# Two of four weight sums of a seven-product matmul moved from VectorE to adding transfers

## The chip, the core and the metric

The kernel runs on one core of a Trainium2 chip. A core has five engines that run their own instruction streams and meet at semaphores: PE (TensorE, matrix products into PSUM), ACT (ScalarE), DVE (VectorE), POOL (GpSimd) and SP (SyncE, which in this kernel only issues transfers). Transfers between HBM and on-chip memory are carried by 16 DMA engines. The metric is the device time of one execution in microseconds, lower is better. The time before is 2126.88 us, the median of three runs (2124.67 to 2127.38).

## What is computed

Two layers of a streaming encoder over 256 positions of width 2048, in float32. The part that the change touches is the MLP of each layer:

```python
def sq_relu_mlp(h, g, w1, w2):
    a = jax.nn.relu(rms_norm(h, g) @ w1)     # 2048 -> 8192
    return (a * a) @ w2                      # 8192 -> 2048

h = h + o.reshape(B, S, D) @ a_w_out[l]
h = h + sq_relu_mlp(h, mlp_norm_g[layer], mlp_w1[layer], mlp_w2[layer])
```

Around it stand a forgetting attention (layer 1), one shared K/V projection, and a chunked attention with a relative bias (layer 2). Every weight is read from HBM once per execution.

## The kernel before

**Products.** A float32 product is made of three passes: weights and activations are each split into a rounded part `hi` and a remainder `lo`, and PE adds up hi times hi, hi times lo and lo times hi (lines 444, 446 and 448). For every weight tile of 128x1024 (a unit), ACT makes `hi` (line 210) and DVE makes `lo` (line 211). A helper, `fetch`, makes these splits for up to two units ahead of the one that PE multiplies, and keeps up to three loads ahead of that. A unit is 12 matmuls of 512 columns.

**Pairs.** The MLP is cut into 4 chunks of 2048 hidden columns. A chunk has four pairs: two that make hidden columns from `w1`, then two (the wide ones, `order == "wide"`) that multiply the hidden activations by `w2`. A pair makes two output blocks of 512 columns for two blocks of 128 positions. There are 16 pairs in each MLP, 32 in all, 16 of them wide. Of the 16 tiles of the inner dimension a pair sends some through a scheme of Strassen's kind, seven products instead of eight, and the rest (units `a2..a7`, `b2..b7`) through the plain way. In a wide pair these are six tiles (1536 weight columns for each quarter), in the others four (1024).

**Forms.** The seven products take the weight matrices 11, T3, T2, T1, 21, T4, 22 in this order (called f0 to f6 in the plan; in a wide pair each has a second, half-size part h0 to h6). 11, 12, 21 and 22 are quarters of the weights, brought from HBM by `bring`. The sums are T3 = 22 - 12, T2 = T3 + 11, T1 = 12 - 11, T4 = 21 - T2, each made by DVE at line 790 (`make`), in the room of a matrix that isn't needed any more: T2 in that of T3, T1 in that of 12, T4 in that of 11. Sums of the activations come from `sums` (lines 271 to 280, tiles `S` and `Sh`).

**Order of a wide pair.** f0 h0, a unit of the pair before (b5), f1 h1, b6, f2 h2, b7, f3 h3, a3, f4 h4, b3, f5 h5, a4, f6 h6, b4, a5, a6, a7; its own b5 to b7 fall into the next pair. T3 is made three or five units ahead of the pair (`prepare`, by the numbers `when`), T2 once T3 has been split (`issue`), T1 after b6, T4 after a3. Within each engine the written order is the order of execution (`keep_order`, for DVE, ACT, PE and SP; POOL isn't in it).

**PSUM.** A pair has four banks, `ps[0][0..1]` for its first block and `ps[1][0..1]` for its second. Before: form 0 goes to `ps[1][0]`, and ACT copies it to `ps[0][0]` (line 879). Form 1 goes to `ps[1][1]`, and ACT copies it to a tile `P7` (line 882), after b6. Forms 2, 3 and 6 go on adding to `ps[1][0]`. After h2 in a wide pair DVE writes `ps[0][1] = ps[1][0] + P7` (line 861), and form 3, which adds to `ps[1][0]`, waits until that has read it. After unit a3 DVE writes `ps[1][1] = ps[1][0] + P7` (line 865).

**Hidden activations.** When a block of hidden columns is complete, DVE turns it in 32x32 blocks (line 314), SP sends it to HBM (`turn<-z`, line 324) and fetches it back in another order (`q<-turn`, line 330). Then `take` makes relu on ACT (line 803), the square rounded to `hi` (808), the square itself (810), and on DVE the remainder `lo` (814, the step called low). These steps run after fixed units of the plan, set by the tuple `uses`, one for each of a chunk's four blocks n = 0 to 3. POOL has no work in the MLP.

Of the kernel before, what the change touches and what calls it, by code (L numbers as in the profile page):

```python
# [11 lines left out]
AF = mybir.ActivationFunctionType  # L12
ALU = mybir.AluOpType
# [19 lines left out]
WIDE = UN + 512  # L33
# [14 lines left out]
def trunk(ctx: ExitStack, tc: tile.TileContext, xT, xr, gs, hg, bf, wgate, w_in, w_oa, w1a, w2fa, w2sa,  # L48
          w_kv, w_qb, w_ob, w1b, w2fb, w2sb, rel, out):
    nc = tc.nc  # L50
    V, S, G, TE, SY = nc.vector, nc.scalar, nc.gpsimd, nc.tensor, nc.sync
# [144 lines left out]
    def issue(parts=1):  # L196
        form = None
        if not raws:
            load(parts)
        raw, cuts = raws.popleft()  # L200
        if not cuts:
            form, half = raw, raw.half
            raw, cuts = form.pair.t[form.name], [slice(0, 512 if half else UN)]
            if half:
                raw = raw[:, UN:]
        n = cuts[-1].stop
        hi = wsp.tile([P, n], F32R, name="hi" if n == UN else "hih", bufs=3 if n == UN else 1)
        lo = wsp.tile([P, n], F32R, name="lo" if n == UN else "loh", bufs=3 if n == UN else 1)
        for c in cuts:
            S.activation(hi[:, c], raw[:, c], AF.Copy)  # L210
            V.tensor_tensor(lo[:, c], raw[:, c], hi[:, c].bitcast(F32), op=ALU.subtract)  # L211
        ready.append((hi, lo, n < UN))
        if form and form.name == "T3" and half == form.pair.wide:
            make(form.pair, "T2")

    def half_next():
        u = raws[0][0] if raws else units[0]
# [29 lines left out]
    part = [None]  # L247
# [14 lines left out]
    def sums(a, fs, n=2):  # L262

        w = [wk.tile([P, 512], F32, name="sum", tag="wk") for _ in range(n)]

        def part(i):
            at = i * n * P
            v = w[at // 512][:, at % 512 : at % 512 + n * P].rearrange("p (g t) -> p g t", g=n)
            return v.rearrange("p g (i c) -> p g i c", i=4) if len(a[0][0].shape) == 4 else v

        V.tensor_tensor(part(0), a[1][0], a[1][1], op=ALU.add)
        V.tensor_tensor(part(1), part(0), a[0][0], op=ALU.subtract)
        V.tensor_tensor(part(2), a[0][0], a[1][0], op=ALU.subtract)
        V.tensor_tensor(part(3), a[0][1], part(1), op=ALU.subtract)
        hi, lo = ([fs[k][:, i * 512 : (i + 1) * 512] for i in range(n)] for k in range(2))
        for i in range(n):
            S.activation(hi[i], w[i], AF.Copy)
        yield
        for i in range(n):
            V.tensor_tensor(lo[i], w[i], hi[i].bitcast(F32), op=ALU.subtract)  # L280
        yield
# [185 lines left out]
    def form_products(ps, hi, lo, x, fs, i, half, stop):  # L467
        items = []
        for g in (2,) if half else range(2):
            if i in (0, 4, 5):  # L470
                xp = [x[2 * g + (i > 0)][:, k, (i == 5) * P : (i == 5) * P + P] for k in range(2)]
            else:
                c = {3: 0, 2: 1, 1: 2, 6: 3}[i]
                c = c * P if half else c * 256 + g * P
                xp = [fs[k + 2 * half][:, c : c + P] for k in range(2)]
            items.append((ps[i not in (4, 5)][i in (1, 5)], xp, g % 2, i < 2 and g == 0, i < 2 and g == stop))
        passes(items, hi, lo, skip_group_check=True)

    def panels(x, evacs, before=None, after=None, which=(None, None), tail=None):
# [301 lines left out]
    def make(p, name):  # L781
        t = p.t
        if name == "T3":
            t[name] = prob.tile([P, 9 * 3 * P], F32, name="wT3", tag="p", bufs=1) if p.order == "early" else room("bias", "wT3")
        else:
            t[name] = t[{"T1": "12", "T2": "T3", "T4": "11"}[name]]
        a, b, op = {"T1": ("12", "11", ALU.subtract), "T3": ("22", "12", ALU.subtract),
                    "T2": ("T3", "11", ALU.add), "T4": ("21", "T2", ALU.subtract)}[name]
        d, a, b = (t[i][:, : WIDE if p.wide else UN] for i in (name, a, b))
        V.tensor_tensor(d, a, b, op=op)  # L790

    def prepare(p, d):
        for name, at in zip(("12", "22", "21", "11", "T3", "T1"), p.units):
# [3 lines left out]
    def mlp(plan, x, Sx, st, last):  # L797
        base = turns[0]
        hids = [[] for _ in range(NCH)]
        Sh = [[] for _ in range(NCH)]  # L800

        def take(t, c, n):
            S.activation(t, t, AF.Relu)
            y = acts.tile([P, 2, GH, T], F32R, name="act")
            hi, lo = (y[:, i].rearrange("p k (b i c) -> p (k b) i c", b=NB, i=4) for i in range(2))
            t3 = t.rearrange("p (i kb c) -> p kb i c", i=4, c=32)
            yield
            S.activation(hi, t3, AF.Square)
            yield
            S.activation(t, t, AF.Square)  # L810
            yield

            def low():
                V.tensor_tensor(lo, t3, hi.bitcast(F32), op=ALU.subtract)  # L814

            hids[c].extend(y[:, :, j, :] for j in range(GH))
            low()
            yield
            if n == 0:
                r = prob.tile([P, 9 * 3 * P], F32R, name="Sh", tag="p", bufs=1)  # L820
                Sh[c].extend(r[:, i : i + n] for i, n in ((0, UN), (UN, UN), (2 * UN, 512), (2 * UN + 512, 512)))
                yield from sums([[t3[:, 2 * j + b :: 4] for j in range(2)] for b in range(NB)], Sh[c])
            elif n == 1:
                yield from sums([[t3[:, 2 * j + b : 2 * j + b + 1] for j in range(2)] for b in range(NB)], Sh[c][2:], 1)

        def turn_hidden(c, n):
            zt = []

            def f(b, ps):
                if b == 0:  # L830
                    zt.extend(turned("q"))
                blocks32(ps, zt[0], b)
                if b == NB - 1:
                    step = steps(lambda: take(zt[1], c, n))
                    uses = ((4, 5, 7, 8, 9, 10), (4, 5, 6, 7, 8, 9), (4, 5, 6, 8), (3, 4, 4, 5))[n]
                    if not c and n < 2:
                        uses = (4, 5, 6, 8, 9, 9) if n else (4, 4, 5, 6, 7, 8)
                    add_fill(carry(*zt, 0)[:2] + [[step] * uses.count(i) for i in range(3, uses[-1] + 1)])
            return f

        pairs = [p for p, q, u in plan if (q, u) == (2, 0)]

        def open_pair(p):
            m = pairs.index(p)
            c, second, r = m // 4, m % 4 >= 2, m % 2
            p.x, p.fs = (hids[c], Sh[c]) if second else (x, Sx)
            p.ps = [acc_pair(base), acc_pair(2 if p.third else 1 - base)]
            if second:
                p.evac = [(last if c == NCH - 1 else residual)(2 * r + q, st.r2) for q in range(2)]
            else:  # L850
                p.evac = [turn_hidden(c, 2 * r + q) for q in range(2)]

        starts = [i for i, it in enumerate(plan) if it[1:] == (2, 0)]
        for i, (p, q, u) in enumerate(plan):
            hi, lo = fetch()
            if p.ps is None:
                open_pair(p)
            if q > 1:
                form_products(p.ps, hi, lo, p.x, p.fs, u, q == 3, 1 + p.wide)
                if u == 2 and q == 2 + p.wide:  # L860
                    V.tensor_tensor(p.ps[0][1], p.ps[1][0], p.t["P7"], op=ALU.add)
            else:
                products(p.ps[q], hi, lo, p.x, u, not units and not ready, p.fast)
                if p.fast and (q, u) == (0, p.own):
                    V.tensor_tensor(p.ps[1][1], p.ps[1][0], p.t["P7"], op=ALU.add)
                    if p.wide:
                        make(p, "T4")
                run_fill()
                if u == KT // UA - 1:
                    for b in range(NB):  # L870
                        p.evac[q](b, p.ps[q][b])
                nxt = next((j for j in starts if j > i), None)
                if nxt is not None:
                    d = sum(1 for it in plan[i:nxt] if it[1] < 2)
                    prepare(plan[nxt][0], d)
            f, kind, k = plan[i - 1]
            if i and kind > 1 and kind == 2 + f.wide and k < 2:
                if k == 0:
                    S.activation(f.ps[0][0], f.ps[1][0], AF.Copy)
                else:  # L880
                    f.t["P7"] = wk.tile([P, 512], F32, name="p7", tag="wk")
                    S.activation(f.t["P7"], f.ps[1][1], AF.Copy)
                    make(f, "T1" if f.wide else "T4")

    st1, x1, S1 = RowStats("m"), [], []
    stage(o, [next_x(n, None, st1, 1, x1, fs=S1, then=st1.inverse if n == NG - 1 else None) for n in range(NG)], tail=tail_a, plan=plan_a)
# [126 lines left out]
```

## Time and profile before

| | |
|---|---|
| median of the runs | 2126.88 us |
| profiled execution, its own time | 2126.07 us |
| its span, first to last instruction | 2124.3 us |
| granted TensorE clock | 0.999 |
| PE busy | 2101.3 us (99%) |
| DVE busy | 1654.6 us (78%) |
| ACT busy | 1211.3 us (57%) |
| POOL busy | 49.1 us (2%) |
| bytes moved by transfers | 491.63 MB |

PE is busy nearly all the time, so what can be won without fewer products is PE's idle time, 23 us over the whole span. The view of waits tells which instruction ended such a wait, and the timeline shows the instructions of an engine in order of time, with the idle time ahead of one in square brackets behind it.

### The profile page before, as it was taken

To read this page: it belongs to the slowest core of one execution; us is meant where nothing else is said; L and a number is where in the kernel's file an instruction comes from. 1 tells how busy PE (TensorE), PEld (TensorE's weight loads), DVE (VectorE), ACT (ScalarE), POOL (GpSimd) and SP (SyncE) were. 2 spreads that over 40 slices of the span, in tenths; PEclk is the share of its full clock that TensorE was granted. 3 is DMA by queue.
4 is the path that set the end of the run, shared out by engine and by line. 5 is a ranking of instruction groups with operands and counts; after the bars stand their busy time and mean duration, and the time that the engine had idled before them with its cause. 6 is when DMAs were issued, how large, how long until landed. Compare 5 with 4: busy or idle time off the path is not lost.

```text
span 2124.3 us, 26113 instructions
## 1 busy us (share of the span) xinstructions
PE 2101.3 (99%) x9278; PEld 1729.3 (81%) x9278; DVE 1654.6 (78%) x1931; ACT 1211.3 (57%) x1519; POOL 49.1 (2%) x48
## 2 busy tenths in 40 slices
PE   9999999999999999999999999999999999999999
PEld 7888888877888887888788888888788878878887
DVE  5767776888788878878877677678887887888786
ACT  6544445665566566556575454456654655665664
POOL 1001000000000000000001010000000000000000
PEclk9999999999999999999999999999999999999999
DMA  8787788776676576477577777787766766765763
GB/s 281 244 249 243 224 264 255 238 246 210 220 256 206 200 265 228 170 239 269 181 240 261 234 228 235 239 276 237 247 211 217 241 203 222 248 212 195 261 234 129
DMA packets 179283, 491.63 MB, mean 231 GB/s; under 512 B 36416, under 2 KB 73424, under 8 KB 179152
## 3 DMA queue, kind: packets, MB, share of 16 engines
q1 hardware_dynamic: 179152, 489.96, 69.8%
q8 instruction: 73, 1.20, 0.2%
q14 instruction: 58, 0.48, 0.1%
HBM read 450.01 MB, written 39.87 MB: 231 GB/s over the span
## 4 chain that ended last, share of the span: by engine, by line
PE 84%; DVE 7%; DMA 4%; ACT 2%; issue 2%; SPq 1%; ACTq 0%; DVEq 0%
PE acc L446 23%; PE acc L448 23%; PE acc L444 23%; PE s L444 4%; PE s L446 4%; PE s L448 4%; DVE lo L211 3%; ACT hi L210 2%; DVE w L790 1%; DVE loh L211 1%; DMA q<-turn 1%; DMA turn<-z 1%; DMA raw<-in_w_in 1%; DVE wT L790 1%; PE s L583 1%
## 5 line engine op out<-in xcount | busy, mean ns | idle before, releaser
L211 DVE TENSOR_TENSOR lo<-raw,hi 128x1024 fp32r<-128x1024 f32 (+1 forms) x610 | 738.2, 1215 | 260.1 <-ACT hi L210 253.0
L210 ACT ACTIVATE hi<-raw 128x1024 fp32r<-128x1024 f32 (+1 forms) x610 | 640.8, 1053 | 367.3 <-PE acc L446 266.8
L444 PE MATMUL acc<-hi,act 128*128 128x512 f32 x2208 | 608.4, 394 | 2.0 <-ACT hi L210 1.1
L446 PE MATMUL acc<-hi,act 128*128 128x512 f32 x2208 | 599.7, 390 | 6.4 <-DVE act L814 6.4
L448 PE MATMUL acc<-lo,act 128*128 128x512 f32 x2208 | 598.4, 390 | 0.0
L446 PEld LDWEIGHTS acc<-hi,act 128*128 128x128 f32 x2208 | 413.4, 188 | 98.2 <-DVE act L814 10.7
L448 PEld LDWEIGHTS acc<-lo,act 128*128 128x128 f32 x2208 | 413.3, 188 | 89.0 <-DVE lo L211 3.2
L444 PEld LDWEIGHTS acc<-hi,act 128*128 128x128 f32 x2208 | 412.9, 188 | 87.9 <-ACT hi L210 2.1
L210 ACT ACTIVATE hi<-w 128x1024 fp32r<-128x1024 f32 x160 | 169.1, 1057 | 226.4 <-DVE w L790 105.2
L211 DVE TENSOR_TENSOR lo<-w,hi 128x1024 fp32r<-128x1024 f32 x160 | 194.8, 1218 | 83.9 <-ACT hi L210 83.8
L444 PE MATMUL s<-hi,act 128*128 128x512 f32 x416 | 112.6, 389 | 0.0
L446 PE MATMUL s<-hi,act 128*128 128x512 f32 x416 | 112.5, 389 | 0.0
L448 PE MATMUL s<-lo,act 128*128 128x512 f32 x416 | 112.5, 389 | 0.0
L210 ACT ACTIVATE hi<-wT 128x1024 fp32r<-128x1024 f32 x64 | 67.7, 1057 | 54.9 <-DVE wT L790 27.9
L448 PEld LDWEIGHTS s<-lo,act 128*128 128x128 f32 x416 | 78.1, 188 | 16.2
L446 PEld LDWEIGHTS s<-hi,act 128*128 128x128 f32 x416 | 78.1, 188 | 16.2
L444 PEld LDWEIGHTS s<-hi,act 128*128 128x128 f32 x416 | 78.0, 188 | 16.2
L211 DVE TENSOR_TENSOR lo<-wT,hi 128x1024 fp32r<-128x1024 f32 x64 | 78.2, 1222 | 9.4 <-ACT hi L210 7.5
L210 ACT ACTIVATE hih<-w 128x512 fp32r<-128x512 f32 x80 | 49.8, 622 | 24.2 <-PE acc L446 16.0
L617 ACT ACTIVATE act<-po 128x256 fp32r<-128x256 f32 x32 | 12.3, 384 | 86.0 <-PE po L615 86.0
L211 DVE TENSOR_TENSOR loh<-w,hih 128x512 fp32r<-128x512 f32 x80 | 54.8, 685 | 7.3 <-ACT hih L210 7.3
L525 POOL TENSOR_TENSOR rn<-vv,mhalf 128x4 f32<-128x4 f32 x32 | 43.3, 1366 | 385.0 <-DVE vv L524 384.9
(190 smaller groups left out, 1717.0 us busy)
## 6 DMA issues: line engine op xcount, KB each, us to landing
raw<-in_w1a SPq DMA_DIRECT2D x96, 512.0 KB, 4.4
raw<-in_w1b SPq DMA_DIRECT2D x96, 512.0 KB, 4.5
raw<-in_w_in SPq DMA_DIRECT2D x94, 512.0 KB, 4.6
raw<-in_w2sa SPq DMA_DIRECT2D x80, 512.0 KB, 4.3
raw<-in_w2sb SPq DMA_DIRECT2D x80, 512.0 KB, 4.2
raw<-in_w_kv SPq DMA_DIRECT2D x64, 512.0 KB, 4.6
turn<-z SPq DMA_DIRECT2D x60, 512.0 KB, 4.2
w<-in_w2fa SPq DMA_DIRECT2D x32, 768.0 KB, 7.6
```

Source lines behind the costliest of these rows:

```text
L210: S.activation(hi[:, c], raw[:, c], AF.Copy)
L211: V.tensor_tensor(lo[:, c], raw[:, c], hi[:, c].bitcast(F32), op=ALU.subtract)
L444: TE.matmul(ps, xh, cut(hi, j), start=first, stop=False, **kw)
L446: TE.matmul(ps, xl, cut(hi, j), start=False, stop=False, **kw)
L448: TE.matmul(ps, xh, cut(lo, j), start=False, stop=last, **kw)
L525: G.tensor_tensor(rn, vv, mhalf, op=ALU.pow)
L583: TE.matmul(s[:, P : 3 * P], q[:, a, P:T], k[:, a], start=True, stop=True)
L617: S.activation(o[i][:, 0], po[:, :T], AF.Copy)
L790: V.tensor_tensor(d, a, b, op=op)
```

## The change

In the wide pairs T1 and T4 are no longer made by DVE. POOL issues a transfer that reads the second operand from HBM and adds it to the tile that is there already (`put`): T1 is 11 added to the tile of 12, issued as soon as T3 is made; T4 is 21 added to the tile of T2, issued when T2 has been split. The quarters 11 and 21 are still brought for their own products, so each is read from HBM twice. An adding transfer can't subtract, so signs are turned: T3 = 22 + 12, T2 = T3 + 11, T1 = 12 + 11, T4 = 21 + T2, for all pairs. The sums of the activations become differences, and two banks change roles: form 0 now goes to `ps[1][1]`, form 1 to `ps[1][0]`. After `P7` is copied from `ps[1][0]`, a further ACT instruction writes minus form 0, from `ps[1][1]`, into `ps[1][0]`, to which form 2 then adds. Line 861 becomes one instruction that turns the sign and subtracts. In the pairs that aren't wide DVE still makes all four sums. Last, the step low of a chunk's fourth block comes one unit earlier (`uses` for n = 3).

```diff
--- before.py
+++ after.py
@@ -210,8 +210,11 @@
             S.activation(hi[:, c], raw[:, c], AF.Copy)
             V.tensor_tensor(lo[:, c], raw[:, c], hi[:, c].bitcast(F32), op=ALU.subtract)
         ready.append((hi, lo, n < UN))
-        if form and form.name == "T3" and half == form.pair.wide:
-            make(form.pair, "T2")
+        if form and half == form.pair.wide:
+            if form.name == "T3":
+                make(form.pair, "T2")
+            elif form.name == "T2" and half:
+                put(form.pair, "T4")
 
     def half_next():
         u = raws[0][0] if raws else units[0]
@@ -268,9 +271,9 @@
             v = w[at // 512][:, at % 512 : at % 512 + n * P].rearrange("p (g t) -> p g t", g=n)
             return v.rearrange("p g (i c) -> p g i c", i=4) if len(a[0][0].shape) == 4 else v
 
-        V.tensor_tensor(part(0), a[1][0], a[1][1], op=ALU.add)
-        V.tensor_tensor(part(1), part(0), a[0][0], op=ALU.subtract)
-        V.tensor_tensor(part(2), a[0][0], a[1][0], op=ALU.subtract)
+        V.tensor_tensor(part(0), a[1][0], a[1][1], op=ALU.subtract)
+        V.tensor_tensor(part(1), a[0][0], part(0), op=ALU.subtract)
+        V.tensor_tensor(part(2), a[1][0], a[0][0], op=ALU.subtract)
         V.tensor_tensor(part(3), a[0][1], part(1), op=ALU.subtract)
         hi, lo = ([fs[k][:, i * 512 : (i + 1) * 512] for i in range(n)] for k in range(2))
         for i in range(n):
@@ -473,7 +476,7 @@
                 c = {3: 0, 2: 1, 1: 2, 6: 3}[i]
                 c = c * P if half else c * 256 + g * P
                 xp = [fs[k + 2 * half][:, c : c + P] for k in range(2)]
-            items.append((ps[i not in (4, 5)][i in (1, 5)], xp, g % 2, i < 2 and g == 0, i < 2 and g == stop))
+            items.append((ps[i not in (4, 5)][i in (0, 5)], xp, g % 2, i < 2 and g == 0, i < 2 and g == stop))
         passes(items, hi, lo, skip_group_check=True)
 
     def panels(x, evacs, before=None, after=None, which=(None, None), tail=None):
@@ -784,10 +787,17 @@
             t[name] = prob.tile([P, 9 * 3 * P], F32, name="wT3", tag="p", bufs=1) if p.order == "early" else room("bias", "wT3")
         else:
             t[name] = t[{"T1": "12", "T2": "T3", "T4": "11"}[name]]
-        a, b, op = {"T1": ("12", "11", ALU.subtract), "T3": ("22", "12", ALU.subtract),
-                    "T2": ("T3", "11", ALU.add), "T4": ("21", "T2", ALU.subtract)}[name]
+        a, b = {"T1": ("12", "11"), "T3": ("22", "12"), "T2": ("T3", "11"), "T4": ("21", "T2")}[name]
         d, a, b = (t[i][:, : WIDE if p.wide else UN] for i in (name, a, b))
-        V.tensor_tensor(d, a, b, op=op)
+        V.tensor_tensor(d, a, b, op=ALU.add)
+        if p.wide and name == "T3":
+            put(p, "T1")
+
+    def put(p, name):
+
+        at, other = {"T1": ("12", "11"), "T4": ("T2", "21")}[name]
+        p.t[name] = p.t[at]
+        G.dma_start(p.t[name][:, :WIDE], p.big[other], accum_op=ALU.add)
 
     def prepare(p, d):
         for name, at in zip(("12", "22", "21", "11", "T3", "T1"), p.units):
@@ -832,7 +842,7 @@
                 blocks32(ps, zt[0], b)
                 if b == NB - 1:
                     step = steps(lambda: take(zt[1], c, n))
-                    uses = ((4, 5, 7, 8, 9, 10), (4, 5, 6, 7, 8, 9), (4, 5, 6, 8), (3, 4, 4, 5))[n]
+                    uses = ((4, 5, 7, 8, 9, 10), (4, 5, 6, 7, 8, 9), (4, 5, 6, 8), (3, 4, 4, 4))[n]
                     if not c and n < 2:
                         uses = (4, 5, 6, 8, 9, 9) if n else (4, 4, 5, 6, 7, 8)
                     add_fill(carry(*zt, 0)[:2] + [[step] * uses.count(i) for i in range(3, uses[-1] + 1)])
@@ -858,13 +868,11 @@
             if q > 1:
                 form_products(p.ps, hi, lo, p.x, p.fs, u, q == 3, 1 + p.wide)
                 if u == 2 and q == 2 + p.wide:
-                    V.tensor_tensor(p.ps[0][1], p.ps[1][0], p.t["P7"], op=ALU.add)
+                    V.scalar_tensor_tensor(p.ps[0][1], p.ps[1][0], -1.0, p.t["P7"], op0=ALU.mult, op1=ALU.subtract)
             else:
                 products(p.ps[q], hi, lo, p.x, u, not units and not ready, p.fast)
                 if p.fast and (q, u) == (0, p.own):
                     V.tensor_tensor(p.ps[1][1], p.ps[1][0], p.t["P7"], op=ALU.add)
-                    if p.wide:
-                        make(p, "T4")
                 run_fill()
                 if u == KT // UA - 1:
                     for b in range(NB):
@@ -876,11 +884,13 @@
             f, kind, k = plan[i - 1]
             if i and kind > 1 and kind == 2 + f.wide and k < 2:
                 if k == 0:
-                    S.activation(f.ps[0][0], f.ps[1][0], AF.Copy)
+                    S.activation(f.ps[0][0], f.ps[1][1], AF.Copy)
                 else:
                     f.t["P7"] = wk.tile([P, 512], F32, name="p7", tag="wk")
-                    S.activation(f.t["P7"], f.ps[1][1], AF.Copy)
-                    make(f, "T1" if f.wide else "T4")
+                    S.activation(f.t["P7"], f.ps[1][0], AF.Copy)
+                    S.activation(f.ps[1][0], f.ps[1][1], AF.Copy, scale=-1.0)
+                    if not f.wide:
+                        make(f, "T4")
 
     st1, x1, S1 = RowStats("m"), [], []
     stage(o, [next_x(n, None, st1, 1, x1, fs=S1, then=st1.inverse if n == NG - 1 else None) for n in range(NG)], tail=tail_a, plan=plan_a)
```

## The prediction

> **What bounds the kernel now.** I read the page's first and third part, then the waits of PE, then the timeline of the wide pairs engine by engine.
>
> ```profile
> span 2124.3 us, 26113 instructions
> ...
> PE 2101.3 (99%) x9278; PEld 1729.3 (81%) x9278; DVE 1654.6 (78%) x1931; ACT 1211.3 (57%) x1519; POOL 49.1 (2%) x48
> ...
> q1 hardware_dynamic: 179152, 489.96, 69.8%
> ```
>
> PE idles 23.0 us in the whole span (2124.3 - 2101.3), and no product goes away. What the change can win at most is the part of these 23 us that lies at the weight sums. The waits of PE (in total, times, longest) say how much that is:
>
> ```profile
> PE acc L446 <- DVE act L814: 6.4, 10, 1.2
> PE s L444 <- DVE acc L861: 5.1, 4, 2.1
> PE acc L444 <- DVE acc L861: 3.6, 4, 1.9
> ```
>
> All three are waits for DVE and together 15.1 us; the rest lies at the start, in the attention and at the end. The longest of them, in the first wide pair:
>
> ```profile
> 470.44 0.62 PE L444 MATMUL s<-hi,Sh 128*128 128x512 f32 x2
> ...
> 471.72 0.58 ACT L882 ACTIVATE p<-s 128x512 f32<-128x512 f32 x1
> ...
> 472.31 1.75 DVE L790 TENSOR_TENSOR w<-w,w 128x1536 f32<-128x1536 f32 x1
> ...
> 474.43 1.06 ACT L210 ACTIVATE hi<-w 128x1024 fp32r<-128x1024 f32 x1 [2.14 <-DVE w L790]
> ...
> 475.52 1.22 DVE L211 TENSOR_TENSOR lo<-w,hi 128x1024 fp32r<-128x1024 f32 x1 [1.47 <-ACT hi L210]
> ...
> 476.66 0.69 DVE L861 TENSOR_TENSOR acc<-s,p 128x512 f32<-128x512 f32 x1
> ...
> 477.50 0.70 PE L444 MATMUL s<-hi,Sh 128*128 128x512 f32 x2 [2.13 <-DVE acc L861]
> ```
>
> L790 makes T1 (1.75 us), ACT can only then split it, DVE idles 1.47 us for that split, and L861, queued behind, comes late for form 3. So 8.7 us (5.1 + 3.6) hang on T1 standing in DVE's order. The 6.4 us at L814, the step low, are of two kinds, one row of each:
>
> ```profile
> 490.77 1.19 PE L446 MATMUL acc<-hi,act 128*128 128x512 f32 x4 [0.56 <-DVE act L814]
> ...
> 502.52 1.20 PE L446 MATMUL acc<-hi,act 128*128 128x512 f32 x4 [1.25 <-DVE act L814]
> ```
>
> The first is block n = 2 in the first wide pair of a chunk: DVE has just made T4 and has idled for its split. The second is block n = 3, the one whose low the change runs a unit earlier.
>
> **The change part by part.**
>
> *T1 and T4 leave DVE: up to -15.1 us.* 32 instructions of 1.75 us, 56 us of DVE, which by itself is worth nothing on an engine that is 78% busy; what counts are the waits above. Without T1 the split at 474.43 needs only ACT, L861 stands right behind h2, and form 3 finds its bank free. Without T4 low of n = 2 comes about 3 us earlier (1.75 and the idle for the split). I take all waits at L861 and those of n = 2. The other end is nothing, if the transfers land no sooner than the sums did.
>
> *low of n = 3 a unit earlier.* Before it low, DVE only needs ACT's square (L810), which the trace shows done at 499.1 in that place, 2 us before low starts; the split that DVE would have done first moves back by one L814 (1.2 us), with a unit of 2.7 us of PE work as cover. It takes the rest of the 6.4 us.
>
> ```profile
> 498.06 1.06 ACT L810 ACTIVATE q<-q 128x1024 f32<-128x1024 f32 x1
> ...
> 501.25 1.22 DVE L814 TENSOR_TENSOR act<-q,act 128x1024 fp32r<-128x1024 f32 x1
> ```
>
> *The sign turned on ACT: +14.5 us.* This is the new wait. Form 2 now adds to a bank that ACT must first have copied to P7 and then overwritten with minus form 0. Before, form 2 waited for neither. I price the second ACT instruction like the copy (0.58 us) and 0.1 us for the handover (a matmul starts 0.15 us after the end of L861 above; consecutive rows of ACT overlap by 0.05). The wait is then: end of P7 + 0.68 - start of form 2 in the trace of before. P7 and form 2 of the first and the last pair of each kind (the first of all, 471.72 and 470.44, stands above; of the third kind one of six equal ones):
>
> ```profile
> 2035.96 0.58 ACT L882 ACTIVATE p<-s 128x512 f32<-128x512 f32 x1
> 2036.21 0.62 PE L444 MATMUL s<-hi,Sh 128*128 128x512 f32 x2
> ...
> 515.51 0.58 ACT L882 ACTIVATE p<-acc 128x512 f32<-128x512 f32 x1
> 516.71 0.61 PE L444 MATMUL acc<-hi,Sh 128*128 128x512 f32 x2
> ...
> 2077.84 0.58 ACT L882 ACTIVATE p<-acc 128x512 f32<-128x512 f32 x1
> 2078.89 0.62 PE L444 MATMUL acc<-hi,Sh 128*128 128x512 f32 x2
> ...
> 598.45 0.58 ACT L882 ACTIVATE p<-acc 128x512 f32<-128x512 f32 x1
> 599.46 0.62 PE L444 MATMUL acc<-hi,S 128*128 128x512 f32 x2
> ```
>
> First wide pair of a chunk: 2.5 (form 2 at 470.44) to 1.0 us; over the eight 11.5 us. Second wide pair: 0.06 in the first and 0.2 in the last, over the eight 1.5 us. Of the 16 other pairs six come out at 0.25, as at 599.46, together 1.5 us, and ten have about half a microsecond to spare. Sum 14.5 us. It is firm, because in the first wide pairs P7 stands in ACT's order behind a split and a square of block n = 2, and this queue starts from PE itself:
>
> ```profile
> 640.29 0.63 ACT L210 ACTIVATE hih<-wT 128x512 fp32r<-128x512 f32 x1 [0.31 <-PE s L446]
> 640.83 1.05 ACT L210 ACTIVATE hi<-raw 128x1024 fp32r<-128x1024 f32 x1
> 641.78 1.04 ACT L808 ACTIVATE act<-q 128x1024 fp32r<-128x1024 f32 x1
> 642.72 0.58 ACT L882 ACTIVATE p<-s 128x512 f32<-128x512 f32 x1
> ```
>
> Behind the new instruction in ACT's queue stands the split of T1, which before waited for DVE anyway (to 474.43), so nothing further is late. Ends: the handover may be 0.1 us more or less in some 20 pairs, 12 to 17 us.
>
> *The adding transfers.* 32 of 768 KB from POOL. The trace shows none; the nearest row is the plain load of the same tile, and the time they have is from the trigger to the split in the trace of before:
>
> ```profile
> w<-in_w2fa SPq DMA_DIRECT2D x32, 768.0 KB, 7.6
> ...
> 622.85 1.75 DVE L790 TENSOR_TENSOR wT<-w,w 128x1536 f32<-128x1536 f32 x1
> ...
> 644.90 1.06 ACT L210 ACTIVATE hi<-w 128x1024 fp32r<-128x1024 f32 x1 [1.59 <-DVE w L790]
> ...
> 641.15 0.69 DVE L211 TENSOR_TENSOR loh<-wT,hih 128x512 fp32r<-128x512 f32 x1
> ...
> 656.00 1.06 ACT L210 ACTIVATE hi<-w 128x1024 fp32r<-128x1024 f32 x1 [4.33 <-DVE w L790]
> ...
> 641.80:656.00 14.20, 14.13 (x62) 11.38 (x62) 12.83 (x14) 7.51 (x10) 0.00 (x0) 1.00 0.54 181
> ```
>
> T1 has 20 us here (624.6 to 644.9), T4 14 us (641.8 to 656.0); in the other wide pairs the least is about 14. Lower end of the price: the plain 7.6. Upper end: every byte counted three times (read, read, written) with all of the plain load's time, 23 us. An engine-bound pass over 786 KB is 2.4 us at the rate while busy (489.96 MB in 69.8% of 2124.3 us, 330 GB/s), so one pass more makes 10 us; I take 10, near the plain row, because the DMA engines are only 0.54 busy in that window. POOL is idle there, so its issue delays nobody. Then T1 and T4 are in time, at no cost.
>
> *Smaller edits, at nothing.* L861 stays one instruction on the same bank, and with T1 gone from DVE it has unit b7 (2.7 us of PE) as cover. T4 now holds T3's room longer, but the next T3 is written by DVE behind T4's split in its own order. The other pairs keep T4 on DVE, where it stood. In SP's queue the next load of 21 no longer waits until T4 has read that tile, which can only help; POOL's waits hold up nothing, as no other work stands in its queue in the MLP.
>
> The Trainium skill (Collectives: The Full Stack, "The bandwidth ceiling: the fold count and why AG ≠ RS ≠ AR") says that an add in the DMA engine costs a second read on the same ring, which halves its rate, and that the add itself costs no cycles. By it the transfer comes to the same 10 us, and not to 23; no run so far shows it.
>
> *What the transfers push aside: +4 us.* T1's transfer of a first wide pair runs beside `turn<-z` and `q<-turn` of block n = 2, for which L803 waits, ahead of the P7 above in ACT's order.
>
> ```profile
> 461.40 2.87 DMA q<-turn
> ...
> 465.94 1.04 ACT L803 ACTIVATE q<-q 128x1024 f32<-128x1024 f32 x1
> ...
> 1860.41 1.06 ACT L803 ACTIVATE q<-q 128x1024 f32<-128x1024 f32 x1 [0.36 <-DMA q<-turn]
> ...
> 1862.47 1.06 ACT L210 ACTIVATE hi<-wT 128x1024 fp32r<-128x1024 f32 x1 [0.51 <-DVE wT L790]
> ```
>
> The slack is between 2 us (the data land at 464.3, and ACT idles a little later) and 0.5 us (pair at 1860, where L803 waits already). If the second pass of 2.4 us delays q by 2 us, the eight pairs lose from 0 to 1.5 us each, about 0.5 in the mean: 4 us. Ends: 0, and 8 x 3 us for a delay of 4 to 5 us.
>
> *Sum.* Against the profiled execution's own time: 2126.07 - 15.1 + 14.5 + 4 = 2129.5; the eight waits at form 3 under 0.1 us that the view of waits leaves out give back 0.6. I predict 2129.0 us. The profiled execution stands 0.8 us under the median of 2126.88, so this is +0.1%, no change: 0.2% is 4.3 us, about what a measurement of this kernel can tell. Own range of this case: 2123 to 2134.
>
> **The rivals.**
>
> *Faster: the wait at form 2 is covered.* If ACT reached P7 a microsecond earlier in the first wide pairs, the 11.5 us fall away, and with low and L861 early the time is 2129 - 11.5 = 2117.5, with no delay of q 2114. For it: DVE has 56 us less to do, and in pair 470 the queue of ACT starts from DVE. Against it: at 640 it starts from PE, and nothing that DVE gives up lies between there and P7. It decides where P7 ends 0.7 us ahead of form 2.
>
> *Slower: q comes late.* A delay of 4 to 5 us costs 8 x 3 us at form 2: 2125 + 24 = 2149. The point is a delay above 2 us. For it: in pair 1860 there is no slack ahead of L803. Against it: DMA is busy for only two thirds of the span. The Trainium skill (DMA: Bandwidth & Descriptors, "Issuing engines are not separate DMA queues") says that transfers from any engine run on the same 16 DMA engines and interleave. By that rule POOL's queue buys no bandwidth and this rival is the one to fear; the trace, with one data queue, can't show it.
>
> *Much slower: the adding transfer takes longer than 14 us.* ACT then stands at the split of T4, and PE at form 5. At 18 us T4 is 4 us late in 16 pairs and T1 in the second wide pairs as much: 2125 + 64 + 32 = 2221. For it: POOL's issue and the add have no row at all. Against it: it needs more than twice the plain 7.6.
>
> **How the numbers follow.** Forecast 0.42, faster rival 0.2, q late 0.28, transfer too long 0.1. Of the forecast I count 0.04 as faster and 0.06 as slower by 0.2%, of the faster rival all but 0.01 as faster: faster 0.23, same 0.33, slower 0.44. The range leaves out the longest transfers and the extreme of the faster rival: 2116 to 2149.
>
> **What would show it.** Right: no waits of PE for L861; low of n = 3 with no wait; new waits of PE at form 2 (`s<-hi,Sh`) for the ACT instruction behind L882, eight of 1.0 to 2.5 us, near 14 us in all; adding transfers that land in some 10 us; splits of T1 and T4 with no idle time for them. Wrong: ACT idle at `hi<-w` for an adding transfer (too long), L803 waiting for q in the first wide pairs (q late), or form 2 starting without a wait. PE's busy time should stay at 2101 us.

## The result and the profile after

The change makes the kernel slower: 2148.57 us (median of four runs, 2146.69 to 2152.65) against 2126.16 us for the kernel before (four runs by now), a ratio of 1.0108 with a 95% interval of 1.0091 to 1.0126. The profiled execution took 2148.78 us.

The page of the changed kernel, with the answer of the view of transfers for those that POOL issues (bytes of each, median us from issue to landing):

```profile
span 2147.0 us, 26205 instructions
...
PE 2108.5 (98%) x9278; PEld 1737.5 (81%) x9278; DVE 1612.2 (75%) x1899; ACT 1234.2 (57%) x1551; POOL 76.9 (4%) x80
...
q1 hardware_dynamic: 179152, 489.96, 68.8%
q0 software_dynamic: 4608, 25.17, 6.8%
```

```profile
w<-in_w2fa POOLq DMA_DIRECT2D x8, 768.0 KB, 9.3
wT<-in_w2fa POOLq DMA_DIRECT2D x8, 768.0 KB, 7.6
w<-in_w2fb POOLq DMA_DIRECT2D x8, 768.0 KB, 8.7
wT<-in_w2fb POOLq DMA_DIRECT2D x8, 768.0 KB, 7.4
```

The span grew by 22.7 us. PE's idle time grew from 23.0 to 38.5 us, which is 15.5 us; the other 7.2 us are PE busy for longer, with the same 9278 matmuls. The transfers themselves land in 7.4 to 9.3 us in the median, each of them in 7.0 to 10.3 us, inside the 14 us they have. The waits of PE (total, times, longest):

```profile
PE s L447 <- ACT s L891: 28.6, 8, 4.7
PE acc L447 <- ACT hi L210: 2.0, 3, 0.9
```

All waits for DVE at the weight sums and at low are gone, and in their place stands one wait, at form 2 of the eight first wide pairs, for the ACT instruction that turns the sign (L891). It is 3.6 us in the mean, and the kernel before had at most 2.1 us at any one of its waits here. The timeline of the pair that the prediction showed at 640 us, first as it was issued before, then after:

```profile
626.99 0.33 SPq L324 DMA_DIRECT2D turn<-z  x1
631.85 1.75 SPq L330 DMA_DIRECT2D q<-turn  x4
```

```profile
629.49 0.86 POOL L800 DMA_DIRECT2D w<-in_w2fa  x1 [108.09 <-DVE wT L792]
...
631.34 0.89 SPq L327 DMA_DIRECT2D turn<-z  x1
641.11 1.75 SPq L333 DMA_DIRECT2D q<-turn  x4
...
645.32 1.06 ACT L813 ACTIVATE q<-q 128x1024 f32<-128x1024 f32 x1 [3.91 <-DMA q<-turn]
646.28 0.58 ACT L887 ACTIVATE acc<-s 128x512 f32<-128x512 f32 x1
646.80 1.04 ACT L210 ACTIVATE hi<-wT 128x1024 fp32r<-128x1024 f32 x1
647.74 0.61 ACT L210 ACTIVATE hih<-wT 128x512 fp32r<-128x512 f32 x1
648.26 1.04 ACT L210 ACTIVATE hi<-raw 128x1024 fp32r<-128x1024 f32 x1
649.21 1.04 ACT L818 ACTIVATE act<-q 128x1024 fp32r<-128x1024 f32 x1
650.15 0.57 ACT L890 ACTIVATE p<-s 128x512 f32<-128x512 f32 x1
650.76 0.58 ACT L891 ACTIVATE s<-s 128x512 f32<-128x512 f32 x1
...
651.39 0.73 PE L447 MATMUL s<-hi,Sh 128*128 128x512 f32 x2 [3.90 <-ACT s L891]
...
657.91 0.61 PE L447 MATMUL s<-hi,Sh 128*128 128x512 f32 x2
```

SP can fetch `q` only when `turn` has landed, so the distance of its two rows is the landing time of `turn<-z`: 4.9 us before, 9.8 us after. T1's transfer starts 1.9 us ahead of it, and from 631.3 to 636.0 us the DMA engines are 0.96 busy, against 0.57 while `turn<-z` was on its way before. Relu (L813) waits 3.9 us for its data, and behind relu in ACT's order stand, without a gap, the copy of form 0 (L887), the splits of T2, a split of a load, the square, P7 and the turned sign. PE waits for the last of them.

Six of the eight first wide pairs are like this one: `turn<-z` lands in 7.8 to 9.8 us, in the kernel before in 4.4 to 5.3 us. In the first of each layer it lands as before, and T1's transfer, issued later, holds back `q<-turn` in its place. The chain of work in the first pair, where the prediction's row for `q<-turn` had 2.87 us:

```profile
458.31 4.40 DMA turn<-z
...
464.32 7.26 DMA q<-turn
```

Then comes something the prediction had no term for. From form 2 to form 3 PE takes 6.5 us in the pair at 640 (651.39 to 657.91), for work that it does in 4.9 us elsewhere. Stretches of the changed kernel, with PE's busy time, the granted clock (PEclk) and the share of the DMA engines (the two numbers ahead of the last):

```profile
646.00:651.30 5.30, 1.49 (x7) 0.91 (x5) 2.96 (x3) 5.27 (x9) 0.87 (x1) 1.00 0.52 208
652.70:656.10 3.40, 3.40 (x10) 2.63 (x9) 2.40 (x4) 1.97 (x3) 0.00 (x0) 0.50 0.96 220
656.20:660.00 3.80, 3.80 (x19) 3.11 (x18) 3.13 (x4) 1.60 (x3) 0.00 (x0) 1.00 0.72 249
823.40:830.10 6.70, 4.30 (x10) 3.43 (x11) 3.12 (x5) 3.76 (x6) 0.87 (x1) 0.50 0.63 116
```

PE is granted half its clock, for 3.4 us in that pair, from 1.3 us behind the end of the wait on, and for 6.8 us in the pair at 823, where the first 2.4 us still lie in the wait (10 matmuls in 3.4 us against 19 in 3.8 us). Six of the eight pairs have such a stretch. From form 2 to form 3 these six take 6.4 to 7.3 us and the two others 4.9 us, 10.5 us more in all.

### The profile page after: what moved, and what is told of

Its sections match the earlier page's. It is cut to its first block, busy times and chain, and to the rows that moved or that the text cites. A ratio compares the mean times of both kernels' runs of the same rounds, so it can differ in the third digit from the quotient of the medians.

```text
span 2147.0 us, 26205 instructions
## 1 busy us (share of the span) xinstructions
PE 2108.5 (98%) x9278; PEld 1737.5 (81%) x9278; DVE 1612.2 (75%) x1899; ACT 1234.2 (57%) x1551; POOL 76.9 (4%) x80
## 3 DMA queue, kind: packets, MB, share of 16 engines
q0 software_dynamic: 4608, 25.17, 6.8%
## 4 chain that ended last, share of the span: by engine, by line
PE 90%; DMA 5%; ACT 3%; issue 1%; DVE 1%; SPq 1%; ACTq 0%
PE acc L447 24%; PE acc L449 23%; PE acc L451 23%; PE s L447 6%; PE s L449 6%; PE s L451 6%; DMA turn<-z 2%; ACT hi L210 1%; DMA q<-turn 1%; DMA raw<-in_w_in 1%; PE s L586 1%; PE po L617 1%; ACT act L818 1%; DMA raw<-in_w1b 0%; DMA raw<-in_w1a 0%
## 5 line engine op out<-in xcount | busy, mean ns | idle before, releaser
L211 DVE TENSOR_TENSOR lo<-w,hi 128x1024 fp32r<-128x1024 f32 x144 | 175.1, 1216 | 75.8 <-ACT hi L210 75.7
L210 ACT ACTIVATE hi<-w 128x1024 fp32r<-128x1024 f32 x144 | 152.5, 1059 | 129.6 <-PE acc L449 57.8
L211 DVE TENSOR_TENSOR lo<-wT,hi 128x1024 fp32r<-128x1024 f32 x80 | 97.6, 1220 | 29.9 <-ACT hi L210 28.7
L210 ACT ACTIVATE hi<-wT 128x1024 fp32r<-128x1024 f32 x80 | 84.5, 1056 | 56.5 <-DVE wT L792 22.4
L210 ACT ACTIVATE hih<-w 128x512 fp32r<-128x512 f32 x64 | 40.2, 628 | 79.4 <-PE acc L449 49.6
L211 DVE TENSOR_TENSOR loh<-w,hih 128x512 fp32r<-128x512 f32 x64 | 44.1, 689 | 21.7 <-ACT hih L210 20.6
```

## The experiments

Theory A: T1's adding transfer holds back `turn<-z`, and through `q`, relu and ACT's order makes form 2 late; the half clock follows from the wait. Theory B: the sign turned on ACT is the loss by itself, and was priced too low. Theory C: it is the bandwidth that both transfers take from the loads. Each ratio below is to the kernel before on the same chip, and it can differ a little from the quotient of the medians. Line numbers are those of each run's own kernel.

**All sums on DVE, signs turned.**

```diff
-            elif form.name == "T2" and half:
-                put(form.pair, "T4")
...
-        if p.wide and name == "T3":
-            put(p, "T1")
...
+                    if p.wide:
+                        make(p, "T4")
...
-                    if not f.wide:
-                        make(f, "T4")
+                    make(f, "T1" if f.wide else "T4")
```

> All four weight sums stay on DVE as plain additions, with the signs and banks of the changed kernel (the extra ACT copy ahead of form 2, low of n = 3 a unit earlier), and no adding transfer. Theory A (T1's transfer holds back turn<-z and so q, relu, P7 and form 2): turn<-z lands in its old 4 to 5 us, PE waits at form 2 for the extra ACT copy by the 14.5 us of the prediction, of which the old waits at L861 in the first wide pairs (5 us) and low of n = 3 (3 us) pay a part: about 2132 us, TensorE clock as before. Theory B (the sign turned on ACT is the loss, larger than was priced): 2145 us or more, form 2 waiting 3 to 4 us in each first wide pair.

Measured: 2129.16 us, ratio 1.0016 (1.0006 to 1.0025). Its waits of PE:

```profile
PE s L445 <- ACT s L889: 9.8, 8, 2.3
PE acc L445 <- ACT acc L889: 3.6, 4, 1.4
PE acc L445 <- DVE acc L867: 2.0, 5, 1.3
```

Form 2 waits for 13.4 us (9.8 in the first wide pairs and 3.6 elsewhere), where the prediction had 14.5 us. Of the old waits for DVE only 2.0 us are left, though DVE still makes all four sums: while PE stands at form 2, DVE has time to catch up (in the runs below without such waits, the waits for DVE are back). So the net loss is 3 us. Theory B falls.

**One of the two transfers at a time.** `t4_only` is the changed kernel with T1 made by DVE, `t1_only` that with T4 made by DVE, each by its part of the diff above.

> T1 is made by DVE at its old place, T4 by the adding transfer; all else as in the changed kernel. Theory A: q of block n = 2 is on time, form 2 waits 1.0 to 2.5 us in the first wide pairs, low of n = 2 without a wait, second wide pairs keep some of L861's waits (4 us): about 2129 us. Theory B: 2145 us or more. Theory C (either transfer costs, by the bandwidth it takes from the loads): about 2137 us, half of the loss.

> T1 by the adding transfer, T4 by DVE at its old place. Theory A: the whole loss stays, about 2148 us, turn<-z of n = 2 lands in some 10 us and form 2 waits 2 to 4.7 us. Theory B: the same time, but then the kernel without transfers has it too. Theory C: about 2137 us.

Measured: 2127.13 us, 1.0004 (0.9991 to 1.0017), with T4's transfer alone, and 2153.16 us, 1.0128 (1.0111 to 1.0145), with T1's alone. The first lines of their waits of PE, each with relu's wait for `q`, first `t4_only`, then `t1_only`:

```profile
PE s L447 <- ACT s L889: 11.4, 8, 2.4
PE acc L447 <- ACT acc L889: 3.1, 3, 1.3
...
ACT q L811 <- DMA q<-turn: 12.0, 10, 2.4
```

```profile
PE s L445 <- ACT s L891: 28.9, 8, 4.0
...
ACT q L811 <- DMA q<-turn: 27.2, 10, 4.0
```

The whole loss hangs on T1's transfer; T4's, as large and as many, costs nothing. In the six pairs `turn<-z` lands in 4.5 to 5.3 us with T4's transfer alone and in 8.7 to 9.8 us with T1's. That is theory A, and theory C falls: it isn't bandwidth as such but which transfer stands beside it.

**PE kept busy through the wait.**

```diff
+            if q == 2 and u == 2 and p.wide and p.third:
+                idle = ps_o.tile([P, 512], F32, name="pt", tag="po")
+                for _ in range(20):
+                    TE.matmul(idle[:, :T], p.x[0][:, 0, :P], p.x[1][:, 0, :], start=True, stop=True)
             if q > 1:
                 form_products(
```

> The changed kernel with 20 idle matmuls of 256 columns (some 2.2 us, into a PSUM tile that nobody reads) ahead of form 2 in the first wide pairs, so that PE works through most of the wait. If the wait itself makes the granted clock fall to half for 3.4 to 6.8 us afterwards, the matmuls behind form 2 run at full speed again, the clock is 0.998 or more and the time about 2148 - 11 = 2138 us. If the clock falls for another reason, or its fall costs nothing on the path, the time stays at 2148 us or rises by up to 2 us.

Measured: 2134.61 us, 1.0048 (1.0033 to 1.0063), 14 us less than the changed kernel, with 160 more matmuls. Its granted clock is 0.999 in the mean, against 0.993 of the changed kernel. From form 1 to form 2 the eight pairs take as long as in the changed kernel, 68.5 against 68.6 us in all, so the wait itself is no shorter; from form 2 to form 3 seven of the eight now take 4.9 us. So the half clock is a consequence of PE standing idle, and it lies on the path. The Trainium skill (TensorE: Matmul & The Clock Gate, "Part 1: The HAM clock gate (the "warmup" mystery)") says that the default clock is half and that activity releases it, in a window of about 3.4 us that runs freely; the stretch of 3.4 us above and this experiment agree. The rule of the Trainium skill against PE-idle gaps above about 3 us (TensorE: Matmul & The Clock Gate, "Why this matters for your kernels") isn't borne out in full: in the changed kernel the stretch comes with waits of 2.3 and 3.9 to 4.7 us, but not with those of 2.0 and 3.2 us.

What sorts these waits is where they lie. The clock records of a trace lie on a grid: from one stretch at half clock to the next it is always a whole number of slices of 3.41 us. Four slices of the changed kernel's grid follow, the two that share the wait of 3.2 us, then that of the wait of 2.0 us, then that of the wait of 2.3 us (the second number is PE's busy time):

```profile
994.02:997.43 3.41, 1.97 (x9) 1.31 (x7) 1.75 (x3) 3.41 (x6) 0.00 (x0) 1.00 0.84 338
997.43:1000.84 3.41, 1.63 (x7) 1.35 (x8) 1.90 (x3) 2.66 (x4) 0.87 (x1) 1.00 0.45 52
1710.82:1714.23 3.41, 1.57 (x7) 0.95 (x6) 2.96 (x3) 3.38 (x6) 0.86 (x1) 1.00 0.33 132
1881.48:1884.89 3.41, 1.08 (x6) 0.58 (x4) 2.83 (x3) 3.38 (x6) 0.86 (x1) 1.00 0.18 73
```

The slices behind the first three ran at full clock, the one behind the last at half. Over all 13 traces of this case (from 60 us on, without the end) 31 slices at full clock are followed by one at half, and in them PE was busy for 0 to 1.57 us; in every other slice at full clock it was busy for 1.56 us or more.

**The two copies ahead of the unit's other ACT steps.** In the MLP's loop, for the unit behind form 1:

```diff
+                f, kind, k = plan[i - 1]
+                if i and kind > 1 and kind == 2 + f.wide and k == 1:
+                    f.t["P7"] = wk.tile([P, 512], F32, name="p7", tag="wk")
+                    S.activation(f.t["P7"], f.ps[1][0], AF.Copy)
+                    S.activation(f.ps[1][0], f.ps[1][1], AF.Copy, scale=-1.0)
                 run_fill()
```

(and the same two gone from their place behind `run_fill`)

> The changed kernel with the two ACT copies (P7 and the turned sign) ahead of that unit's other ACT steps (the rounded square L818 of block n = 2) instead of behind them. Theory A: q is still late and relu still stands ahead of the copies in ACT's order, so that only the square's 1.0 us goes from each wait at form 2: some 8 us, and a part of the half clock, about 2137 us. If ACT's order were the whole cause the waits would be gone: about 2115 us.

Measured: 2134.11 us, 1.005 (1.0032 to 1.0068). The first line of its waits, from an execution of 2127.55 us, the fastest of its ten:

```profile
PE s L447 <- ACT s L880: 17.6, 8, 2.9
```

The square's place was worth 11 us of waits (28.6 to 17.6) by this execution, where 8 were expected; as the median is 6.6 us longer, a typical one has probably won less. The rest stays, as relu still waits for `q`, for 28.9 us in all against 27.9 us in the changed kernel.

**The same transfers without the add.**

```diff
-        G.dma_start(p.t[name][:, :WIDE], p.big[other], accum_op=ALU.add)
+        G.dma_start(p.t[name][:, :WIDE], p.big[other])
```

> The changed kernel with plain loads in the place of the adding transfers, from POOL's queue, of the same bytes: the additions are left out, so T1 is 11 and T4 is 21. If the second pass of the adding transfer holds back turn<-z, the plain load lands in 7 to 8 us, turn<-z in some 7, form 2 waits about half as long: about 2133 us. If any transfer of 768 KB on a second queue does it, the time stays at about 2148 us.

Measured: 2134.55 us, 1.003 (1.0012 to 1.0048). Its queue of POOL and T1's landing times, from the view of transfers, then its waits:

```profile
q0 software_dynamic: 4608, 25.17, 3.5%
...
w<-in_w2fa POOLq DMA_DIRECT2D x8, 768.0 KB, 6.1
...
w<-in_w2fb POOLq DMA_DIRECT2D x8, 768.0 KB, 6.0
```

```profile
PE s L447 <- ACT s L891: 18.6, 8, 3.5
```

For the same 25.17 MB the add doubles what the 16 DMA engines are busy with it (6.8% against 3.5% of the span) and adds 3 us to the landing. So half the rate, by the rule of the Trainium skill that the prediction quotes, agrees with these runs; the second read itself no view shows. Without the add 10 of the 28.6 us at form 2 go. What is left, 18.6 us, is above the 9.8 us (`signs_only`) and 11.4 us (`t4_only`) of the same eight waits without T1's transfer: a plain load at that place still pushes `turn<-z` aside, to 6.2 to 8.0 us in the six pairs.

**Low of n = 3 alone.** The kernel before with `(3, 4, 4, 4)` in `uses`.

> The kernel before with low of n = 3 one unit earlier and nothing else. The three long waits at low of n = 3 (2.8 us in the trace of before) go: about 2123 us. If the earlier step holds up a split on DVE instead, no change or slower.

Measured: 2127.13 us, 1.0002 (0.999 to 1.0015): nothing. Its waits of PE:

```profile
PE acc L444 <- DVE acc L861: 6.1, 7, 2.6
PE s L444 <- DVE acc L861: 5.4, 4, 2.2
PE acc L446 <- DVE act L814: 3.6, 7, 0.5
```

The waits at low fall by 2.8 us, as expected, and those at L861 rise by the same 2.8 us (8.7 to 11.5): the time moved to the next late thing.

**T1's transfer only in the second wide pairs.** `p7_first`, with T1 made by DVE in the first wide pair of a chunk:

```diff
         if p.wide and name == "T3":
-            put(p, "T1")
+            if not p.third:
+                put(p, "T1")
...
-                    if not f.wide:
-                        make(f, "T4")
+                    if not f.wide or f.third:
+                        make(f, "T1" if f.wide else "T4")
```

> T1 by DVE in the first wide pair of each chunk and by the transfer in the second, T4 by the transfer in both, and the two ACT copies ahead of the unit's other ACT steps. Theory A: q on time, form 2 without a wait in the first wide pairs, no waits at low, L861 only in first wide pairs (5.4 us before): 2126 - 15 + 5 = 2116 us, faster than both kernels by 0.4%. If T1's transfer hurts the second wide pairs too, 2130 us or more.

Measured: 2115.03 us, 0.9943 (0.9927 to 0.9959), faster than both kernels. Waits of PE:

```profile
PE acc L447 <- ACT acc L881: 4.2, 6, 1.3
PE s L447 <- ACT s L881: 3.7, 4, 1.4
```

The time is the one expected, but not by the waits expected: L861's line has 0.3 us in place of 5.4, and form 2 still waits for ACT, for 7.9 us (4.2 + 3.7). In the second wide pairs T1's transfer also takes 8.5 to 9.8 us to land, but no instruction that PE waits for is late for it.

**The same order of copies without transfers.** `signs_only` with the edit of `p7_first`.

> signs_only with the two ACT copies ahead of the unit's other ACT steps, no adding transfer. Form 2 waits for about 7 us instead of 13, and some waits of L861 come back, as PE is no longer held up before them: about 2123 us. If moving the copies alone made combo fast, 2116 us.

Measured: 2125.06 us, 0.9984 (0.9972 to 0.9997). That is 1.4 us below the kernel before on the same chip, and `combo` is 11 us below it. Moving the copies isn't what makes `combo` fast; it needs the transfers.

**Form 1 in a free bank.** `combo`, with form 1 sent to `ps[0][1]`, so that the sign can be turned right behind form 0:

```diff
-            items.append((ps[i not in (4, 5)][i in (0, 5)], xp, g % 2, i < 2 and g == 0, i < 2 and g == stop))
+            items.append((ps[i not in (1, 4, 5)][i in (0, 1, 5)], xp, g % 2, i < 2 and g == 0, i < 2 and g == stop))
...
-                    S.activation(f.t["P7"], f.ps[1][0], AF.Copy)
-                    S.activation(f.ps[1][0], f.ps[1][1], AF.Copy, scale=-1.0)
+                    S.activation(f.t["P7"], f.ps[0][1], AF.Copy)
...
+                    S.activation(f.ps[1][0], f.ps[1][1], AF.Copy, scale=-1.0)
                     S.activation(f.ps[0][0], f.ps[1][1], AF.Copy)
...
+                if p is pairs[0]:
+                    TE.matmul(p.ps[1][0], p.x[0][:, 0, :P], hi[:, :512], start=True, stop=True)
```

(the first new copy stands behind form 1, the second behind form 0; the matmul writes the whole bank once in each MLP, since nothing else there now starts an accumulation in it)

> combo, with form 1 in the bank ps[0][1], which is free until line L871 writes it, and the turned sign of form 0 written into ps[1][0] by ACT right behind form 0 instead of behind P7. Form 2 then waits for nothing new. If the wait at form 2 is all that is left, combo's 7.9 us of it go: about 2107 us. If ACT's one further copy behind form 0 makes the splits of T3 or T2 late, 2110 us or more.

> The same banks with all four sums made by DVE and no adding transfer. What the transfers are worth by themselves, once nothing else is in the way: if the waits at L861 and at low of n = 2 come from T1 and T4 in DVE's order, some 10 us of them are back and the time is 2116 to 2119 us; if the transfers give nothing, as banks.

Measured: `banks` 2109.85 us, 0.9907 (0.9887 to 0.9927), the best of all; `banks_dve` 2125.02 us, 0.9991 (0.9977 to 1.0004), a miss of 6 us. Waits of PE, first `banks`, then `banks_dve`:

```profile
PE s L447 <- DVE acc L874: 4.4, 3, 1.9
```

```profile
PE acc L445 <- DVE acc L869: 6.1, 7, 1.6
PE s L445 <- DVE acc L869: 4.6, 3, 1.8
PE acc L447 <- DVE act L820: 3.6, 7, 0.5
```

Nothing waits for ACT at form 2 any more. What `banks` has left, 4.4 us at the old place, are three first wide pairs, where T1 is still in DVE's order. Without the transfers the waits for DVE are 14.3 us, 10 us more, as expected, but the two kernels differ by 15 us: that is what 24 adding transfers are worth when nothing else is in their way. Where the other 5 us come from is not shown; PE's busy time is 3.9 us longer without the transfers (2100.5 against 2096.6 us).

## Why the prediction was wrong

Predicted 2129.0 us and no change; measured 2148.57 us, inside the range by half a microsecond, and at the time of the rival "q comes late", which named 2149 us with a chance of 0.28.

- *T1 and T4 leave DVE, -15.1 us.* Right as a number, as these waits are gone, but it isn't the transfers that took most of them. In `signs_only`, with all four sums on DVE, 13 of the 15.1 us are gone too, paid by the wait at form 2: the sum's first two terms are not independent. The worth of the transfers shows where form 2 doesn't wait, in `banks` against `banks_dve`: 10 us of waits and 15 us of time.
- *low of n = 3.* Right as to its waits, which went. Alone it gives nothing (`uses_only`), as L861 then waits for as much more.
- *The sign turned on ACT, +14.5 us.* Right: 13.4 us in `signs_only`, of them 9.8 in the first wide pairs, where the sum had 11.5.
- *The adding transfers in 10 us and in time.* Right: 7.4 to 9.3 us in the median, no split waits for one.
- *What the transfers push aside, +4 us.* This step failed, in its size. It charged `q` with the add's second pass alone, 2 us. Measured over the six pairs, `turn<-z` lands 4 us later in the mean (9.0 against 5.0 us), and with plain loads already 2.5 us later (7.5 us): the first pass, which the sum put at nothing, is the larger part. Its upper end, a delay of 4 to 5 us, is about what came. Against it the prediction had set that DMA is busy for only two thirds of the span; at the moment `turn<-z` ran, the DMA engines were 0.96 busy. The wait at form 2 of the first wide pairs came to 28.6 us, where the sum had 15.5 us (11.5 + 4); the 3 us that it had at the other pairs didn't come, so the waits are 10 us more than the sum's 18.5.
- *A missing term.* The sum charged a wait of PE with its own length only, and the prediction expected PE's busy time to stay at 2101 us; it is 2108.5 us. Against the profiled execution the forecast is 19.3 us short (2148.78 - 2129.5). 10 us are waits, and the 9 us left fit the half clock behind them, which is 7.2 us by PE's busy time, 10.5 us by the stretches from form 2 to form 3, and 14 us by `keep_warm`. So the rival reached the right number with a part of the wrong reasons: its 24 us were all waits, and the runs show fewer waits and slower matmuls. That its number came out so closely is luck.

## What to carry to other kernels

Before a transfer is added, look which transfer that something waits for runs in the same few microseconds, and price the new one by what lands late there, not by the DMA engines' mean share; here one of two equal transfers cost 24 us (`t1_only` against `signs_only`) and the other nothing. Where PE waits for about 2 us or more, count the half clock that can follow as well as the wait; in these traces it came when PE was busy for less than about 1.6 us of a slice of 3.41 us. And put an instruction on which PE depends ahead of its engine's other work, or give it a bank in which it can run earlier: the same idea went from 1.1% slower to 0.9% faster by that and by dropping eight of the 32 transfers.

## What the runs showed of the hardware

An adding transfer of 768 KB takes POOL about 0.86 us to issue and lands in 7.0 to 10.3 us, where a plain one from the same queue took 4.4 to 8.3 us. It occupies the DMA engines twice as long as a plain one of the same bytes (6.8% against 3.5% of the span for 32). While T1's ran, a transfer of 512 KB from SP's queue took 7.8 to 9.8 us to land in six pairs, in place of 4.4 to 5.3 us. With eight waits of PE of 2.0 to 4.7 us the granted clock fell to 0.50 in six cases, for 3.4 or 6.8 us; it did so behind a slice of 3.41 us in which PE was busy for 1.3 us or less (in all 13 traces 1.57 us or less).
